# A fused two-block model kernel on one core: GpSimd's conv taps in halves, and a planner of orders with added latency and a noisy replay

## The chip, the cores and the metric

The kernel runs on one core of a Trainium2 chip. The core has five engines with queues of their own that run in order: TensorE (PE, matmuls and transposes), VectorE (DVE), ScalarE (ACT), GpSimd (POOL) and SyncE (SP, which issues DMAs; GpSimd issues some too). The metric is the device time of one execution in microseconds.

## The reference

The reference takes 512 tokens of width 1024 in float32 through two models, one behind the other. The first is one layer: an RMS norm, a mixer (a projection, a causal convolution of 4 taps, an SSD scan in chunks of 128 for 16 heads, a pooling over windows of 2 to 16 tokens, a projection), a cross-attention over 256 memory rows, a SwiGLU of width 2816, and a final norm. The second has two layers. Layer A is the one that the change touches:

```python
def conformer_conv(u, conv_w, conv_b, g, b):
    a, gl = jnp.split(u, 2, axis=-1)
    h = a * jax.nn.sigmoid(gl)
    h = jnp.pad(h, ((0, 0), (CONV_KERNEL - 1, 0), (0, 0)))      # CONV_KERNEL = 31, width 1536
    h = depthwise_conv(h, conv_w) + conv_b
    return jax.nn.silu(layer_norm(h, g, b))
```

Its output and a cross-attention over another 256 memory rows are gated, projected by `a_w_out` and added to the input, and a layer norm follows. Layer B replaces the convolution by an attention in which each query keeps the 256 keys with the best index scores.

## The kernel before, in words

Activations lie transposed, with 128 channels on the partitions and 512 tokens along a row, so one tile is 128x512. Every dense product is made of three float32r matmuls for each 128x128 block (high times high, high times low, low times high): `mm3`, called by `dense`. Weights come in through `prep` (L490): SyncE loads a raw tile (3 buffers), ScalarE rounds it to the high half, and the low half is the difference, made on VectorE with both inputs in SBUF. For the four weights named in `ADDED` (those of layer A's input projection) ScalarE writes the negated high half instead and GpSimd issues a DMA that adds the raw weight to it in SBUF.

`conv_tile` (L1190) makes one of the 12 tiles of layer A's convolution: two dense products (gate and value), the padded product `pad` on VectorE, and 31 taps. Tap 0 is scaled on ScalarE into `cg`. Taps 1 to 10 are scaled on ScalarE into a temporary `tm` each and added to `cg` by GpSimd. Tap 11 is a matmul with a diagonal, into PSUM (`cp`). Taps 12 to 30 are multiply-adds on VectorE with one input in SBUF and one in PSUM. Then `cg` and `cp` are added on VectorE, and the layer norm's running sums go to GpSimd. Beside these 12 tiles run `side` steps: the query and gate projections, the cross-attention, and a part of the output projection.

The body doesn't issue instructions. `Program.rec` (L138) records each as an `Op` with its engine, its tiles, its dependences by whole tile and an estimated duration in ns. `emit` (L402) then makes an order. `order` (L236) is a list scheduler: it walks through time, starts on each engine the ready op of least priority value, and counts the free buffers of each tag; an op is ready at its last producer's end plus `latency` (the table `LATENCY` at L53, by pair of engines). The first order takes its priorities from the program's sequence. Then `latest` (L199) walks an order backwards and gives each op a due time, the priorities become the mean of due times and old start times, and `order` runs again, 12 times (`FBI`). `replay` (L366) walks a finished sequence op by op and estimates its length; the shortest of the 13 is issued. Nothing of this runs on the chip: the chip sees only the sequence of each engine's queue, with the semaphores that the dependences need. An op flagged `port` (GpSimd's, and VectorE's where both inputs are in SBUF or the copy is a fast one) waits in the plan until the flagged op that runs on the other of the two engines has ended.

All recorded instructions are issued at L423, so the profile names them by tile and shape.

Of the kernel before, what the change touches and what calls it, by code (L numbers as in the profile page):

```python
# [26 lines left out]
SLOPES = [2.0 ** (-(i + 1)) for i in range(8)] + [2.0 ** (-0.5 * (2 * i + 1)) for i in range(4)]  # L27
BIG = 1e30
WAHEAD = 400
ADDED = ("a_gl", "a_a", "a_qm", "a_gate")  # L30
WINDOW = 1500
SSD = 600
# [10 lines left out]
for _k, _w in _VEC:  # L43
# [5 lines left out]


ENGINES = ("PE", "ACT", "DVE", "POOL", "SP")
SWITCH, FBI, LATE, REUSE, MIX = 40000, 12, 1500, 160, 0.5
LATENCY = {("PE", "PE"): 0.0, ("ACT", "ACT"): 0.0, ("DVE", "DVE"): 130.0, ("POOL", "POOL"): 102.0,  # L53
           ("PE", "ACT"): 200.0, ("PE", "DVE"): 196.0, ("ACT", "PE"): 260.0, ("DVE", "PE"): 300.0, ("POOL", "PE"): 200.0,
           ("ACT", "DVE"): 142.0, ("DVE", "ACT"): 130.0, ("ACT", "POOL"): 175.0, ("DVE", "POOL"): 190.0,
           ("POOL", "ACT"): 75.0, ("POOL", "DVE"): 60.0}
# [66 lines left out]
class Program:  # L123
# [14 lines left out]
    def rec(s, eng, fn, m, args, kw):  # L138
        o = Op()
        o.m = m  # L140
        o.eng, o.fn, o.args, o.kw, o.idx = eng, fn, args, kw, len(s.ops)
        o.prio = o.idx - s.shift
        o.outs = [args[0]] + ([kw["accum_out"]] if kw.get("accum_out") is not None else [])
        o.outs = [x.base for x in o.outs if isinstance(x, View)]
        ins = [x for x in list(args[1:]) + [v for k, v in kw.items() if k != "accum_out"] if isinstance(x, View)]
        o.ins = [x.base for x in ins]
        o.tiles = set(o.outs + o.ins)
        deps = set()
        for x in o.ins:
            if x.writer is not None:  # L150
                deps.add(x.writer)
            x.readers.append(o.idx)
        for x in o.outs:
            if x.writer is not None:
                deps.add(x.writer)
            deps.update(x.readers)
            x.writer, x.readers = o.idx, []
        deps.discard(o.idx)
        o.deps, o.succ = deps, []
        o.new = [x for x in dict.fromkeys(o.outs) if x.alloc is not None and x.left == 0]  # L160
        for x in o.tiles:
            x.left += 1
        o.port, o.table = False, None
        out = args[0]
        n = int(np.prod(out.shape[1:]))
        if eng == "PE":
            one = m == "transpose" or args[1].base.dt == F32R
            o.table = n > 8
            o.dur = 109.0 if m == "transpose" else max(112.0, n / 2.4 + 16) if one else 2 * max(111.0, n / 1.2 + 2)
        elif eng == "ACT":  # L170
            ptr = sum(isinstance(kw.get(k), View) for k in ("scale", "bias", "accum_out"))
            o.dur = n * 0.833 + 93 + 93 * ptr - 40 * (isinstance(args[1], View) and args[1].base.psum)
            o.table = _TABLE.get(args[2])
        elif eng == "DVE":
            two = m in ("tensor_tensor", "scalar_tensor_tensor")
            psum = any(x.psum for x in o.tiles)
            wide = [x for x in ins if int(np.prod(x.shape[1:])) > 1]
            ptr = len(ins) - len(wide)
            if m == "reciprocal":
                o.dur = n * 8.3 + 60  # L180
            elif m in ("tensor_reduce", "max", "match_replace"):
                o.dur = int(np.prod(wide[-1].shape[1:])) * 1.042 + 68
            elif not two and not psum:
                o.dur, o.port = n * 0.521 + 68 + 61 * ptr, n > 8
            else:
                o.dur = n * 1.042 + 68 + 61 * min(ptr, 1)
                o.port = two and sum(not x.base.psum for x in wide) == 2 and n > 8
        elif m == "dma_start" and eng == "POOL":
            o.dur, o.bytes = 1100.0, n * int(out.shape[0]) * 8 / 360.0
        elif eng == "POOL":  # L190
            o.dur, o.port = (1000 if kw.get("op") == ALU.pow else n * (2.35 if len(ins) > 1 else 1.0) + 99), n > 8
        else:
            o.dur = n * int(out.shape[0]) * 4 / 360.0
        s.ops.append(o)

    def latency(s, a, b):
        return LATENCY.get((a.eng, b.eng), 120.0)

    def latest(s, prio):  # L199

        ops = s.ops
        need = [len(o.succ) for o in ops]
        when = [0.0] * len(ops)
        ready = {e: [] for e in ENGINES}
        wait = [(0.0, -prio[o.idx], o.idx) for o in ops if not o.succ]
        heapq.heapify(wait)
        busy = dict.fromkeys(ENGINES, 0.0)
        events, port = [0.0], 0.0
        while events:
            now = heapq.heappop(events)  # L210
            while wait and wait[0][0] <= now:
                _, p, k = heapq.heappop(wait)
                heapq.heappush(ready[ops[k].eng], (p, k))
            for e, q in ready.items():
                if busy[e] > now or not q:
                    continue
                o = ops[q[0][1]]
                if o.port and port > now:
                    heapq.heappush(events, port)
                    continue  # L220
                heapq.heappop(q)
                end = now + (o.dur + 2150 if e == "SP" else o.dur + o.bytes + 2150 if o.m == "dma_start" else o.dur)
                busy[e] = now + o.dur
                if o.port:
                    port = end
                heapq.heappush(events, busy[e])
                when[o.idx] = -end
                for d in o.deps:
                    when[d] = max(when[d], end + s.latency(ops[d], o))
                    need[d] -= 1  # L230
                    if need[d] == 0:
                        heapq.heappush(wait, (when[d], -prio[d], d))
                        heapq.heappush(events, when[d])
        return when

    def order(s, prio, window):  # L236
# [28 lines left out]
        while len(seq) < len(ops):  # L265
# [5 lines left out]
            while fin and fin[0][0] <= now:  # L271
                o = ops[heapq.heappop(fin)[1]]
                for x in o.tiles:
                    left[x] -= 1
                    if left[x] == 0 and x.alloc is not None:
                        back.append((now + REUSE, x))
                        heapq.heappush(events, now + REUSE)
                for k in o.succ:
                    need[k] -= 1
                    rdy[k] = max(rdy[k], o.end + s.latency(o, ops[k]))  # L280
                    if need[k] == 0:
                        heapq.heappush(early, k)
            while back and back[0][0] <= now:
# [79 lines left out]
                    low += 1  # L363
        return seq, max(o.end for o in ops), [o.start for o in ops]

    def replay(s, seq):  # L366

        free, end, left = dict.fromkeys(ENGINES, 0.0), {}, {}
        back, taken, last = {g: [] for g in s.bufs}, dict.fromkeys(s.bufs, 0), {}
        port, hw, dma = {"POOL": 0.0, "DVE": 0.0}, 0.0, 0.0  # L370
        for o in seq:
            for x in o.tiles:
                left[x] = left.get(x, 0) + 1
        for o in seq:
            now = free[o.eng]
            for d in o.deps:
                now = max(now, end[d] + s.latency(s.ops[d], o))
            for x in o.new:
                taken[x.tag] += 1
                if taken[x.tag] > s.bufs[x.tag]:  # L380
                    now = max(now, heapq.heappop(back[x.tag]) + REUSE)
            if o.port:
                now = max(now, port["DVE" if o.eng == "POOL" else "POOL"])
            free[o.eng] = fin = now + o.dur
            if o.eng == "SP":
                hw = max(now, hw) + 470
                dma = max(hw + 650, dma) + o.dur
                fin, free["SP"] = dma + LATE, now + 470
            elif o.m == "dma_start":
                dma = max(fin + 650, dma) + o.bytes  # L390
                fin = dma + LATE
            if o.port:
                port[o.eng] = fin
            end[o.idx] = fin
            for x in o.tiles:
                left[x] -= 1
                last[x] = max(last.get(x, 0.0), fin)
                if left[x] == 0 and x.alloc is not None:
                    heapq.heappush(back[x.tag], last[x])
        return max(end.values())  # L400

    def emit(s, window):  # L402
        def real(a):
# [4 lines left out]
                s.ops[d].succ.append(o.idx)  # L408
        prio = [o.prio * 200.0 for o in s.ops]
        r = s.order(prio, window)  # L410
        best, least = r, s.replay(r[0])
        for it in range(FBI):
            w = s.latest(r[2])
            m = min(w)
            w = [MIX * (t - m) + (1 - MIX) * p for t, p in zip(w, r[2])]
            r = s.order(w, window)
            t = s.replay(r[0])
            if t < least:
                best, least = r, t
        for o in best[0]:  # L420
# [5 lines left out]
def body(ctx, tc, t, out):  # L426
# [763 lines left out]
    def conv_tile(j):  # L1190
# [14 lines left out]
        for k in range(1, NOFF):  # L1205
            tm = act(tag="tm")
            S.activation(tm, tap(k)[0], AF.Copy, scale=tap(k)[1])
            G.tensor_tensor(cg, cg, tm, op=ALU.add)
        cp = bank("B")
        if NPE:  # L1210
            for k in range(NPE):
# [378 lines left out]
```

## Time and profile before

| | us |
|---|---|
| median of 3 runs | 1716.03 |
| lowest and highest of them | 1715.26, 1717.04 |
| the profiled execution | 1714.29 |
| its span, first to last instruction | 1712.5 |
| TensorE busy in it | 1653.5 |
| VectorE busy | 1102.8 |
| ScalarE busy | 811.5 |
| GpSimd busy | 422.6 |

The profile gives the busy time of each engine, for the whole span or for stretches of it, the granted TensorE clock (1.00 is 2.4 GHz, 0.50 is 1.2 GHz), groups of instructions by form (shape) with their mean duration, and a timeline in which instructions of one form that follow each other stand in one row with their count. A bracket behind a row is the time for which the engine had nothing to do before it, and the engine and tile that ended this. A matmul's recorded duration is longer than its share of a full pipeline, so a busy TensorE isn't always one at its peak.

### The profile page before, as it was taken

How to read it: one execution, taken by the hardware profiler on the slowest of the kernel's cores; microseconds unless marked ns; L12 is line 12 of the kernel's file. 1: busy time of each engine (PE TensorE's matmuls, PEld its weight loads, DVE VectorE, ACT ScalarE, POOL GpSimd, SP SyncE). 2: the span in 40 equal slices, each digit the busy share in tenths (PEclk: the TensorE clock that was granted, in tenths of full speed). 3: DMA queues.
4: the chain of work that ended last, by engine and by line, in shares of the span. 5: the costliest groups of instructions: out<-in, count | busy, mean ns of one | idle time of the engine just before them, and what ended most of it. 6: DMA issues, size and time to landing. Idle time of an engine off the chain costs nothing. (4 is left out here: it accounts for less than half of the span.)

```text
span 1712.5 us, 21259 instructions
## 1 busy us (share of the span) xinstructions
PE 1653.5 (97%) x7950; PEld 1353.6 (79%) x7950; DVE 1102.8 (64%) x1761; ACT 811.5 (47%) x1394; POOL 422.6 (25%) x369
## 2 busy tenths in 40 slices
PE   9999998999999999999999987899799999999998
PEld 7888688888888888888888765678687788788886
DVE  7846968554664445644465996886647895467754
ACT  6623544335543222422476894674435425545541
POOL 1003532110221001101345896686230000000000
PEclk9999999999999999999999998999999999999999
DMA  7321224321333332222498625575233123111121
GB/s 235 122 86 56 93 74 125 128 92 38 111 111 99 99 98 91 95 99 78 138 219 175 142 44 132 148 166 139 97 116 114 62 87 123 61 64 50 50 86 50
DMA packets 56055, 179.39 MB, mean 105 GB/s; under 512 B 6352, under 2 KB 8272, under 8 KB 55952
## 3 DMA queue, kind: packets, MB, share of 16 engines
q1 hardware_dynamic: 49616, 154.96, 28.1%
q0 software_dynamic: 6336, 23.07, 7.6%
q8 instruction: 63, 1.03, 0.2%
q14 instruction: 40, 0.33, 0.1%
HBM read 175.78 MB, written 2.10 MB: 104 GB/s over the span
## 5 line engine op out<-in xcount | busy, mean ns | idle before, releaser
L423 PE MATMUL mm<-act,whi 128*128 128x512 f32 (+1 forms) x3888 | 1194.1, 388 | 23.8 <-DVE act L423 12.5
L423 PEld LDWEIGHTS mm<-act,whi 128*128 128x128 f32 x3888 | 720.8, 189 | 177.5 <-DVE act L423 17.3
L423 PE MATMUL mm<-act,wlo 128*128 128x512 f32 (+1 forms) x1944 | 747.5, 387 | 10.1 <-DVE wlo L423 9.9
L423 ACT ACTIVATE whi<-raw 128x1024 fp32r<-128x1024 f32 (+3 forms) x293 | 289.5, 990 | 550.4 <-PE mm L423 365.5
L423 POOL TENSOR_TENSOR act<-act,act 128x512 f32<-128x512 f32 (+1 forms) x252 | 349.9, 1437 | 625.5 <-DVE act L423 329.0
L423 PEld LDWEIGHTS mm<-act,wlo 128*128 128x128 f32 x1944 | 367.8, 189 | 84.9 <-DVE wlo L423 12.4
L423 DVE TENSOR_TENSOR wlo<-raw,whi 128x1024 fp32r<-128x1024 f32 (+3 forms) x249 | 321.8, 1294 | 121.6 <-ACT whi L423 116.7
L423 DVE TENSOR_TENSOR act<-mm,act 128x512 f32<-128x512 f32 (+3 forms) x173 | 114.6, 663 | 240.2 <-PE mm L423 234.2
L423 ACT ACTIVATE act<-act 128x512 fp32r<-128x512 f32 (+3 forms) x222 | 134.2, 617 | 130.7 <-DVE act L423 93.8
L423 DVE SCALAR_TENSOR_TENSOR B<-pad,vec,B 128x512 f32<-128x512 f32 x228 | 168.6, 753 | 11.3 <-PE B L423 6.2
L423 DVE TENSOR_TENSOR act<-act,act 128x512 f32<-128x512 f32 (+3 forms) x203 | 144.9, 742 | 32.3 <-ACT act L423 29.0
L423 POOL TENSOR_TENSOR fr<-fv,mhalf 128x1 f32<-128x1 f32 x4 | 2.2, 546 | 412.2 <-DVE fv L423 412.2
L423 PE MATMUL A<-act,act 128*128 128x256 f32 (+6 forms) x488 | 99.3, 345 | 0.6 <-ACT act L423 0.4
L423 ACT ACTIVATE act<-pad,vec 128x512 f32<-128x512 f32 x144 | 97.3, 737 | 3.0 <-DVE pad L423 2.9
L423 PEld LDWEIGHTS A<-act,act 128*128 128x128 f32 (+1 forms) x488 | 72.3, 190 | 19.7 <-issue 6.1
L423 PE MATMUL mm<-whi,act 128*128 128x512 f32 x264 | 84.3, 393 | 0.0
L423 ACT ACTIVATE act<-C 128x128 f32<-128x128 f32 (+4 forms) x164 | 52.0, 362 | 54.1 <-PE C L423 52.6
L423 PE MATMUL B<-act,act 128*128 128x128 f32 (+1 forms) x492 | 60.1, 290 | 5.4 <-DVE act L423 5.2
L423 PEld LDWEIGHTS B<-act,act 128*128 128x128 f32 (+1 forms) x492 | 50.8, 170 | 14.3 <-DVE act L423 6.3
L423 PE MATMUL C<-ident,act 128*128 128x128 f32 (+1 forms) x288 | 50.0, 279 | 9.1 <-ACT act L423 8.5
L423 PEld LDWEIGHTS mm<-whi,act 128*128 128x128 f32 x264 | 49.4, 188 | 9.6
L423 ACT ACTIVATE act<-act,vec 128x512 fp32r<-128x512 f32 (+3 forms) x68 | 46.4, 700 | 22.3 <-DVE act L423 20.8
(137 smaller groups left out, 1046.6 us busy)
## 6 DMA issues: line engine op xcount, KB each, us to landing
raw<-in_w_g_dram SPq DMA_DIRECT2D x22, 512.0 KB, 3.3
raw<-in_w_u_dram SPq DMA_DIRECT2D x22, 512.0 KB, 3.3
raw<-in_w_om_dram SPq DMA_DIRECT2D x16, 512.0 KB, 4.5
raw<-in_w_d_dram SPq DMA_DIRECT2D x16, 512.0 KB, 3.5
raw<-in_a_gate_dram SPq DMA_DIRECT2D x16, 512.0 KB, 5.5
wlo<-in_a_gate_dram POOLq DMA_DIRECT2D x16, 512.0 KB, 7.8
raw<-in_b_gate_dram SPq DMA_DIRECT2D x16, 512.0 KB, 3.3
raw<-in_b_wo_dram SPq DMA_DIRECT2D x16, 512.0 KB, 3.3
```

What stands on the lines that cost most here:

```text
L423: r = o.fn(*[real(a) for a in o.args], **{k: real(v) for k, v in o.kw.items()})
```

## The change

Three things are changed.

In `conv_tile` each of GpSimd's adds of a tap, 128x512, becomes two adds of 128x256, of the left and the right half of the columns.

The planner's numbers are changed: GpSimd's add of n columns costs 2.3 n + 80 ns (2.35 n + 99 before), a dependent GpSimd instruction has no added latency (102 ns before), the issue of an adding DMA costs 900 ns (1100 before), and its transfer 9.2 / 360 ns a 128-partition element (8 / 360 before). A load is taken to land after 1300 ns instead of 1500. There are 14 rounds instead of 12.

The planner itself is changed in two ways. `order` and `latest` use `planned`, which is the latency plus 300 ns (`SLACK`) where the two ops are on different engines. And `replay` now keeps a queue for each engine and always starts the queue head that can start first, with buffers waited for by the tiles that held them (`slots`), and with each duration but TensorE's multiplied by 1 plus 3% of the absolute value of a normal draw; `emit` judges an order by the sum over three such draws.

```diff
-SWITCH, FBI, LATE, REUSE, MIX = 40000, 12, 1500, 160, 0.5
+SWITCH, FBI, LATE, REUSE, MIX = 40000, 14, 1300, 160, 0.5
+NOISE = 3
+SLACK = 300.0
-LATENCY = {..., ("POOL", "POOL"): 102.0,
+LATENCY = {..., ("POOL", "POOL"): 0.0,
...
         elif m == "dma_start" and eng == "POOL":
-            o.dur, o.bytes = 1100.0, n * int(out.shape[0]) * 8 / 360.0
+            o.dur, o.bytes = 900.0, n * int(out.shape[0]) * 9.2 / 360.0
         elif eng == "POOL":
-            o.dur, o.port = (1000 if kw.get("op") == ALU.pow else n * (2.35 if len(ins) > 1 else 1.0) + 99), n > 8
+            o.dur, o.port = (1000 if kw.get("op") == ALU.pow else n * (2.3 if len(ins) > 1 else 1.0) + 80), n > 8
...
+    def planned(s, a, b):
+        return s.latency(a, b) + (SLACK if a.eng != b.eng else 0.0)
...
-                    when[d] = max(when[d], end + s.latency(ops[d], o))
+                    when[d] = max(when[d], end + s.planned(ops[d], o))
...
-                    rdy[k] = max(rdy[k], o.end + s.latency(o, ops[k]))
+                    rdy[k] = max(rdy[k], o.end + s.planned(o, ops[k]))
...
+    def replay(s, seq, wait, noise):
...
+            for e in live:
+                o = todo[e][0]
+                if e not in head:
+                    if any(end[d] is None for d in o.deps) or any(end[d] is None for d in wait.get(o.idx, ())):
+                        continue
+                    t = [end[d] + s.latency(ops[d], o) for d in o.deps] + [end[d] + REUSE for d in wait.get(o.idx, ())]
+                    head[e] = max(t, default=0.0)
+                t = max(head[e], free[e])
+                if o.port:
+                    t = max(t, port["DVE" if e == "POOL" else "POOL"])
+                if best is None or t < best[0]:
+                    best = (t, e)
+            now, e = best
...
+            free[e] = fin = now + o.dur * (1.0 if e == "PE" else noise[o.idx])
...
-        best, least = r, s.replay(r[0])
+        rng = np.random.default_rng(0)
+        noise = 1.0 + 0.03 * np.abs(rng.standard_normal((NOISE, len(s.ops))))
+        def judge(seq):
+            wait = s.slots(seq)
+            return sum(s.replay(seq, wait, x) for x in noise)
+        best, least = r, judge(r[0])
...
         for k in range(1, NOFF):
             tm = act(tag="tm")
             S.activation(tm, tap(k)[0], AF.Copy, scale=tap(k)[1])
-            G.tensor_tensor(cg, cg, tm, op=ALU.add)
+            for o in (0, T // 2):
+                G.tensor_tensor(cg[:, o:o + T // 2], cg[:, o:o + T // 2], tm[:, o:o + T // 2], op=ALU.add)
```

## Rows read from the trace of the kernel before

**Rows 1.** The page's head and its busy times, share of span, and counts.

```profile
span 1712.5 us, 21259 instructions
PE 1653.5 (97%) x7950; PEld 1353.6 (79%) x7950; DVE 1102.8 (64%) x1761; ACT 811.5 (47%) x1394; POOL 422.6 (25%) x369
```

**Rows 2.** Table by stage: stretch, length, busy us by engine, granted clock, DMA.

```profile
213.00:300.00 87.00, 81.86 (x571) 71.23 (x570) 68.53 (x103) 39.92 (x61) 22.05 (x17) 0.98 0.33 102
300.00:941.00 641.00, 640.17 (x2955) 531.81 (x2954) 335.04 (x419) 267.08 (x413) 118.47 (x100) 1.00 0.38 111
941.00:1037.00 96.00, 82.21 (x355) 61.26 (x354) 93.25 (x146) 82.61 (x176) 84.99 (x74) 0.96 0.39 84
1037.00:1113.00 76.00, 63.53 (x246) 48.95 (x247) 55.10 (x61) 42.96 (x60) 51.64 (x44) 0.89 0.64 157
...
1199.00:1242.00 43.00, 34.30 (x173) 28.60 (x172) 28.83 (x35) 18.98 (x32) 8.77 (x6) 0.92 0.28 97
1242.00:1307.00 65.00, 62.49 (x287) 50.78 (x285) 38.21 (x51) 28.40 (x38) 16.82 (x11) 1.00 0.33 108
1307.00:1696.00 389.00, 388.81 (x1986) 320.80 (x1986) 261.60 (x615) 174.96 (x387) 1.10 (x2) 1.00 0.22 74
1696.00:1712.50 16.50, 8.02 (x36) 6.31 (x34) 8.13 (x18) 3.04 (x8) 1.08 (x2) 0.89 0.17 65
```

**Rows 3.** The same table for the five stretches at the lower clock, with their sum.

```profile
272.00:275.40 3.40, 3.40 (x28) 3.07 (x23) 3.37 (x6) 1.36 (x4) 1.66 (x1) 0.51 0.02 5
...
1074.10:1080.90 6.80, 3.20 (x8) 2.53 (x9) 6.48 (x5) 0.00 (x0) 2.99 (x3) 0.50 0.10 39
1207.30:1214.00 6.70, 3.96 (x17) 3.70 (x17) 4.46 (x4) 6.70 (x13) 2.58 (x2) 0.50 0.04 14
sum 33.80, PE 22.04 PEld 16.97 DVE 31.07 ACT 14.00 POOL 18.06; mean PE 4.41 PEld 3.39 DVE 6.21 ACT 2.80 POOL 3.61
```

**Rows 4.** Timeline of TensorE: its three longest waits (start, us, what, idle before).

```profile
1038.94 1.65 PE L423 MATMUL mm<-act,whi 128*128 128x512 f32 x3 [6.56 <-DVE act L423]
...
1077.70 0.80 PE L423 MATMUL mm<-act,wlo 128*128 128x512 f32 x1 [8.21 <-DVE wlo L423]
...
1210.04 0.80 PE L423 MATMUL mm<-act,whi 128*128 128x256 f32 x2 [5.34 <-ACT act L423]
```

**Rows 5.** Timeline around the second of them, GpSimd and VectorE.

```profile
1067.29 1.19 POOL L423 DMA_DIRECT2D wlo<-in_a_a_dram  x1
...
1067.90 9.19 POOL L423 TENSOR_TENSOR act<-act,act 128x512 f32<-128x512 f32 x7
...
1068.36 9.29 DVE L423 TENSOR_TENSOR wlo<-raw,whi 128x512 fp32r<-128x512 f32 x1
```

**Rows 6.** Table by stage for most of the conv tiles.

```profile
940.00:1180.00 240.00, 212.26 (x904) 164.24 (x903) 192.48 (x269) 168.49 (x294) 191.06 (x164) 0.95 0.60 137
```

**Rows 7.** Groups by form, VectorE, same stretch: busy, mean ns, idle before.

```profile
L423 DVE TENSOR_TENSOR wlo<-raw,whi 128x512 fp32r<-128x512 f32 x8 | 16.3, 2062 | 0.0
L423 DVE TENSOR_TENSOR act<-act,act 128x512 fp32r<-128x512 f32 x8 | 8.1, 1056 | 0.0
...
L423 DVE TENSOR_TENSOR act<-act,act 128x512 f32<-128x512 f32 x5 | 3.3, 689 | 6.1 <-ACT act L423 3.9 <-POOL act L423 2.2
```

**Rows 8.** Timeline of GpSimd: two runs of adds.

```profile
998.51 8.16 POOL L423 TENSOR_TENSOR act<-act,act 128x512 f32<-128x512 f32 x6
...
1018.98 11.09 POOL L423 TENSOR_TENSOR act<-act,act 128x512 f32<-128x512 f32 x9 [0.84 <-ACT act L423]
```

**Rows 9.** Groups by form, GpSimd, 940 to 1180 us.

```profile
L423 POOL DMA_DIRECT2D wlo<-in_a_gl_dram x8 | 7.0, 878 | 4.6 <-ACT wlo L423 4.6
...
L423 POOL MEMSET pad<- 128x30 f32 x6 | 0.7, 124 | 6.5 <-DVE B L423 6.5
```

**Rows 10.** Timeline of GpSimd: a copy and an add into one tile.

```profile
138.27 0.19 POOL L423 COPY act<-act 128x1 f32<-128x1 f32 x1 [4.71 <-DVE act L423]
138.41 1.04 POOL L423 TENSOR_TENSOR act<-act 128x511 f32<-128x511 f32 x1
```

More of the change, by code (lines that the diff above doesn't have):

```diff
@@ L51 @@
 ENGINES = ("PE", "ACT", "DVE", "POOL", "SP")
-SWITCH, FBI, LATE, REUSE, MIX = 40000, 12, 1500, 160, 0.5
-LATENCY = {("PE", "PE"): 0.0, ("ACT", "ACT"): 0.0, ("DVE", "DVE"): 130.0, ("POOL", "POOL"): 102.0,
+SWITCH, FBI, LATE, REUSE, MIX = 40000, 14, 1300, 160, 0.5
+LATENCY = {("PE", "PE"): 0.0, ("ACT", "ACT"): 0.0, ("DVE", "DVE"): 130.0, ("POOL", "POOL"): 0.0,
            ("PE", "ACT"): 200.0, ("PE", "DVE"): 196.0, ("ACT", "PE"): 260.0, ("DVE", "PE"): 300.0, ("POOL", "PE"): 200.0,
@@ L364, in order, with slots @@
         return seq, max(o.end for o in ops), [o.start for o in ops]
[L366 to L370, printed above, removed]
+    def slots(s, seq):
+        left, users, wait = {}, {}, {}
+        back, taken = {g: deque() for g in s.bufs}, dict.fromkeys(s.bufs, 0)
         for o in seq:
@@ L374, in replay @@
         for o in seq:
-            now = free[o.eng]
-            for d in o.deps:
-                now = max(now, end[d] + s.latency(s.ops[d], o))
             for x in o.new:
@@ L380, in replay @@
                 if taken[x.tag] > s.bufs[x.tag]:
[L381 to L385, printed above, removed]
+                    wait.setdefault(o.idx, []).extend(users[back[x.tag].popleft()])
+            for x in o.tiles:
+                users.setdefault(x, []).append(o.idx)
+                left[x] -= 1
+                if left[x] == 0 and x.alloc is not None:
+                    back[x.tag].append(x)
+        return wait
+    def replay(s, seq, wait, noise):
+        ops, end, head = s.ops, [None] * len(s.ops), {}
+        todo = {e: deque(o for o in seq if o.eng == e) for e in ENGINES}
+        free, port, hw, dma = dict.fromkeys(ENGINES, 0.0), {"POOL": 0.0, "DVE": 0.0}, 0.0, 0.0
+        live = [e for e in ENGINES if todo[e]]
+        while live:
+            best = None
+            for e in live:
[11 more added lines that the diff above has]
+            now, e = best
+            del head[e]
+            o = todo[e].popleft()
+            if not todo[e]:
+                live.remove(e)
+            free[e] = fin = now + o.dur * (1.0 if e == "PE" else noise[o.idx])
+            if e == "SP":
                 hw = max(now, hw) + 470
                 dma = max(hw + 650, dma) + o.dur
-                fin, free["SP"] = dma + LATE, now + 470
+                fin, free[e] = dma + LATE, now + 470
             elif o.m == "dma_start":
@@ L392, in replay @@
             if o.port:
-                port[o.eng] = fin
+                port[e] = fin
             end[o.idx] = fin
[L395 to L400, printed above, removed]
+        return max(end)
     def emit(s, window):
@@ L416, in emit @@
             r = s.order(w, window)
-            t = s.replay(r[0])
+            t = judge(r[0])
             if t < least:
```

## The prediction, made before the change was run

> **What bounds the kernel now.** I read the page's busy times first. TensorE holds 1653.5 us of a span of 1712.5 [rows 1], so the most that any order of the same work can give is what TensorE loses: 59.0 us without an instruction, and what it loses at the lower clock. The reader is to see next, in the table by stage, that this loss is not spread out. From 300 to 941 us TensorE is idle for 0.8 us and from 1307 to 1696 for 0.2 [rows 2]: there every order is as good as another. The idle time lies at 213 to 300 (87.00 − 81.86 = 5.1 us, the SSD heads), at 941 to 1037 (13.8) and 1037 to 1113 (12.5), which are the first two thirds of the twelve conv tiles, at 1199 to 1242 (8.7, the layer norm after them), at 1242 to 1307 (2.5) and at the very end (8.5, the closing chain and the output) [rows 2].
>
> Third, the clock. Five stretches inside the kernel run at a granted clock of 0.50, so at 1.2 GHz and not 2.4; each begins during or behind an idle or thinly filled stretch of TensorE. Together they last 33.8 us and TensorE is busy in 22.0 of them; at full clock the same work would take half, so they cost 11.0 us [rows 3].
>
> Fourth, what ended the waits. The three longest are 6.56 us for an activation's low half from VectorE, 8.21 us for a weight's low half from VectorE, and 5.34 us for an evacuation on ScalarE [rows 4]. All three are in-order queues: the producer stood behind other work. The second is of a kind of its own. A VectorE subtraction of 128x512 with both inputs in SBUF took 9.29 us, from 1068.36 on, while GpSimd ran seven adds back to back from 1067.90 to 1077.09 [rows 5]. Its kind takes 0.69 us (the last group there) when nothing is in its way [rows 7]. VectorE got in between none of the seven adds.
>
> No engine is full over the whole conv stage: of 240 us, TensorE holds 212, VectorE 192, GpSimd 191, ScalarE 168 [rows 6]. VectorE alone is full in its first part (93.3 of 96.0 us, 941 to 1037) [rows 2]. So the stage is bound by the order in which four loaded in-order queues hand work to each other, and the order is what the change makes anew.
>
> **The change, part by part.**
>
> (1) *Taps in halves.* Ten adds on each of 12 tiles, 120 adds of 128x512, become 240 of 128x256. No row shows a half. A run of six adds takes 8.16 us, 1.36 each, and a run of nine 11.09, 1.23 each [rows 8]; I read the first as one tile's chain, where an add waits for the one before it, and the second as two chains mixed. An instruction with next to nothing to do, the memset of 30 columns, takes 0.124 us [rows 9]. A half is then between 1.23 / 2 = 0.615 (no fixed part) and (1.23 − 0.124) / 2 + 0.124 = 0.677 us, and two halves 1.23 to 1.35. Against a waiting add that is −0.13 to −0.01, against a mixed one 0 to +0.12: over 120 taps −16 to +14 us of GpSimd. I take 0, since runs of both kinds occur. The cover is GpSimd's idle time, 240.0 − 191.1 = 48.9 us of the stage [rows 6]; only with that gone would these microseconds reach TensorE through the sums.
>
> (2) *Who waits for the halves.* The two halves of one tap touch different columns, so they need not wait for each other, and the first half of the next tap finds its input finished one instruction ago. That GpSimd starts on another slice of a tile without waiting is in the trace: the add of 511 columns begins 0.14 us after a copy of 0.19 us into the same tile began [rows 10]. So a chain that stopped between adds (1.36) would run without a stop, as mixed ones do (1.23). That is good for GpSimd and bad for a VectorE instruction with two SBUF inputs, if rows 5 are the pattern. The stage has 8 + 8 + 5 = 21 such instructions, 27.7 us in all, where 21 × 0.69 would be 14.5 [rows 7]: 13.2 us of waiting, 8.6 of it in the one. The other twenty waited 0.2 us on average, many of them with no add in their way. One locked-out instruction costs TensorE 8.2 us of idle time [rows 4] and half of the 3.2 us that it was busy at the lower clock behind it (1.6) [rows 3], 9.8 us together. What the halves make of their number I bound by none left (−9.8) and four more (+39). I take half a one more, +5: the runs become tighter, but the planner moves the 21 instructions at the same time.
>
> [...]
>
> (3) *The planner.* The numbers in its tables cost nothing on the chip. Three kinds of edit decide the order. Each hop between engines counts 300 ns more, so a consumer is planned later behind its producer and other ready work goes in between. The replay that picks among the orders (now 15 instead of 13) starts each engine's queue head in order of time and sums three runs with durations up to some per cent longer, so an order that only just fits loses. And the costs on GpSimd's queue come nearer to the rows: a DMA's issue 0.9 instead of 1.1 us, measured 0.878 [rows 9]; an add of 512 columns 1.26 instead of 1.30 plus 0.10 for a dependent one, measured 1.23 and 1.36 [rows 8]. "Longer adding DMAs" is such a cost too; no transfer changes.
>
> What that can win: the idle time of the five stretches named above is 5.1 + 13.8 + 12.5 + 8.7 + 2.5 = 42.6 us [rows 2]; without the 8.2 of the lockout, of which the planner expects one add's length at most, 34.4. The start and the end (8.5) are chains that no order shortens. Nothing in the trace shows an order with slack, so its share lies between 0 and 34.4. The nearest rows for the upper end are the calm stages, where work stands far ahead and the loss is 1.0 us in 1030 [rows 2]; for the lower end, the full VectorE of 941 to 1037, where no order makes VectorE's 93 us shorter, only moves them. I take half, −17.2. The lower clock goes with the idle time: of its 11.0 us the lockout holds 1.6; half of the other 9.4 is −4.7.
>
> What is late next: with the 300 ns more, SBUF tiles are planned to live longer, and the 73 buffers of the `act` tag may come free later; loads of weights, which go through three raw buffers, stay where their buffers come free.
>
> **Sum.** −17.2 − 4.7 + 5 + 0 = −16.9 us on the profiled execution of 1714.29: 1697.4. That execution stands 1.74 us under the median of the runs (1716.03), so the forecast is 1699 us.
>
> **The rivals.**
>
> *Lockouts take the gain and more.* Speaking for it: rows 5, and that halves remove the stops between dependent adds. Against: twenty of 21 got in. The price is 9.8 us for each further one. With the planner's −21.9 kept, it decides from the third further one on (2.2 × 9.8 = 21.9). With four: −21.9 + 39.2 = +17.3, so 1733 us.
>
> *Slack spoils the calm stages.* An order built for late hops keeps more tiles alive and lets TensorE idle where it does not now. If the 1030 us of the calm stages came to lose as much as 1242 to 1307 does (2.5 of 65.0, 3.9%) [rows 2], that is +40 less the 1.0 there now; with −16.9 elsewhere +22, so 1738 us. Against it: those stages have VectorE at 335 of 641 us and 262 of 389, far from full.
>
> *Halves let VectorE in.* If VectorE waits for one GpSimd instruction at a time, which the twenty short waits allow and rows 5 deny, a wait ends after a half, at most 0.68 us, and no lockout is left: −17.2 − 4.7 − 9.8 = −31.7, so 1684 us.
>
> *Nearly all is won.* The three long waits of rows 4 go, three quarters of 34.4 and of 9.4 are recovered and no lockout is left: −25.8 − 7.1 − 9.8 = −42.7, so 1673 us.
>
> *The change does not do what it says.* If the halves wait for one another as whole tiles do, each pays the 0.13 us between the two pitches of rows 8, 240 × 0.13 = 31 us on GpSimd instead of nothing; 48.9 us of idle time hold most of it, but half reaching TensorE (+15.6) eats the gain: about 1715 us, within 0.2%. The same time results if the new order only moves the waits about.
>
> **How the numbers follow.** A measurement of this kernel can tell about 0.2% from no change, 3.4 us, so "same" is 1712.6 to 1719.5. Chances: the forecast's case, a part of the loss recovered, 0.40, with 1686 to 1712.6 as its own range; VectorE let in by the halves 0.14; nearly all won 0.10; no change 0.10; lockouts 0.17; calm stages spoiled 0.09. Faster is 0.40 + 0.14 + 0.10 = 0.64, same 0.10, slower 0.26. The range for 8 in 10 goes from 1676, which leaves out most of the best case, to 1736, which takes in the four further lockouts and leaves out the worse of both slow cases.
>
> **What would show it.** In the profile after, GpSimd has 240 adds of 128x256; a mean pitch between 0.61 and 0.68 us confirms (1), one near 0.75 says that halves wait. The longest VectorE subtraction with two SBUF inputs tells (2): none over 2 us says that halves let VectorE in, several over 4 us are the lockout rival. TensorE's idle time between the start of the conv tiles and the end of their layer norm, some 35 us now, should fall to about 18 for (3), and the stretches at half clock from 33.8 to about 20 us. More than 3 us of idle time in the calm stages is the slack rival. The forecast is wrong if VectorE's full stretch, not the order, made the idle time: then VectorE is again full for some 90 us and TensorE's loss beside it is the same.

## The result: slower by 1.6%, and the profile after

The changed kernel takes 1742.39 us (median of 4 runs, 1740.94 to 1747.62) where the kernel before takes 1715.99; the ratio is 1.0159, with a 95% interval of 1.0137 to 1.0181. The forecast was 1699 us, with a range up to 1736. Ratios are taken over fast executions alone, medians over all; two kernels below have one slow execution each (2760.3 us in the new planner without the halves, 1859.95 in the slack alone).

The page's head and busy times of the kernel after answer [rows 1]. The matmuls are the same 7950. The span is 28.7 us longer, and TensorE's idle time grows from 59.0 to 1741.2 − 1659.7 = 81.5 us.

```profile
span 1741.2 us, 21393 instructions
PE 1659.7 (95%) x7950; PEld 1358.9 (78%) x7950; DVE 1136.3 (65%) x1761; ACT 817.8 (47%) x1398; POOL 441.4 (25%) x489
```

The table by stage of the kernel after (stretch, length, busy us of PE, PEld, DVE, ACT and POOL with counts, granted clock, DMA) answers [rows 2], and its last row, a sum over the nine stretches at the lower clock (granted 0.50 to 0.51), [rows 3].

```profile
300.00:860.00 560.00, 560.00 (x2610) 468.51 (x2610) 284.29 (x351) 211.39 (x337) 78.41 (x59) 1.00 0.31 99
...
950.00:1045.00 95.00, 73.29 (x299) 57.32 (x299) 84.38 (x102) 65.26 (x121) 66.42 (x95) 0.87 0.51 114
1045.00:1150.00 105.00, 85.52 (x323) 63.63 (x322) 90.77 (x90) 51.84 (x95) 75.07 (x92) 0.89 0.41 99
1150.00:1250.00 100.00, 88.62 (x411) 71.78 (x410) 75.31 (x92) 62.26 (x89) 70.06 (x70) 0.98 0.54 132
...
1340.00:1724.00 384.00, 383.96 (x1972) 317.10 (x1971) 257.88 (x610) 174.66 (x384) 1.11 (x2) 1.00 0.22 74
...
sum 54.40, PE 39.55 PEld 30.17 DVE 44.98 ACT 24.64 POOL 21.96; mean PE 4.39 PEld 3.35 DVE 5.00 ACT 2.74 POOL 2.44
```

The calm stages are as calm as before. Most of the added loss is in the conv tiles and the layer norm after them: 21.7, 19.5 and 11.4 us of TensorE's idle time in three stretches of some 100 us, 52.6 together, where the stage from 941 to 1242 us lost 36.4 before (13.79 + 12.47 + 8.70 by [rows 2], and 1.48 in the stretch left out there). If half the clock means half the pace, an estimate from the granted 0.50, the lower clock costs half of the 39.6 us that TensorE was busy in it, 19.8, where it cost 11.0. In the traces of both kernels matmuls of 512 columns mostly start 0.427 us apart in these stretches (1.2 columns a ns; the views give the clock as a share only) and 0.227 us apart at 1.00, so by the matmuls it is 47% rather than half.

The timeline of VectorE in the kernel after (start, us, what, idle before), its longest instructions, answers the third row of [rows 5]:

```profile
959.03 3.53 DVE L457 TENSOR_SCALAR xm<-xm 128x2 f32<-128x2 f32 x1
...
987.09 6.90 DVE L457 TENSOR_SCALAR xm<-xm 128x2 f32<-128x2 f32 x1
...
1017.42 9.85 DVE L457 TENSOR_SCALAR xm<-xm 128x2 f32<-128x2 f32 x1
...
1067.81 8.66 DVE L457 TENSOR_TENSOR act<-act,act 128x512 fp32r<-128x512 f32 x2
...
1100.02 5.05 DVE L457 TENSOR_TENSOR wlo<-raw,whi 128x512 fp32r<-128x512 f32 x1 [3.34 <-PE mm L457]
...
1126.16 15.94 DVE L457 TENSOR_TENSOR wlo<-raw,whi 128x512 fp32r<-128x512 f32 x1
```

The first three scale two columns of maxima, an instruction whose quickest copy takes 0.16 us. The fourth row holds two instructions; the long one is the second, 7.79 us. Together the six rows take 49.9 us; undisturbed they would take about 3 (four subtractions at 0.69, three scalings at 0.16). GpSimd's timeline beside them, kernel after:

```profile
958.67 0.80 POOL L457 DMA_DIRECT2D wlo<-in_a_a_dram  x1
959.29 2.96 POOL L457 TENSOR_TENSOR act<-act,act 128x256 f32<-128x256 f32 x4
...
986.21 0.81 POOL L457 DMA_DIRECT2D wlo<-in_a_gl_dram  x1
986.82 7.14 POOL L457 TENSOR_TENSOR act<-act,act 128x256 f32<-128x256 f32 x10
...
1016.20 1.00 POOL L457 DMA_DIRECT2D wlo<-in_a_gl_dram  x1
1016.82 9.43 POOL L457 TENSOR_TENSOR act<-act,act 128x256 f32<-128x256 f32 x13
...
1068.08 0.97 POOL L457 DMA_DIRECT2D wlo<-in_a_gate_dram  x1
1068.69 7.22 POOL L457 TENSOR_TENSOR act<-act,act 128x256 f32<-128x256 f32 x10
...
1125.66 0.87 POOL L457 DMA_DIRECT2D wlo<-in_a_a_dram  x1
1126.28 9.23 POOL L457 TENSOR_TENSOR act<-act,act 128x256 f32<-128x256 f32 x13
1135.27 1.08 POOL L457 DMA_DIRECT2D wlo<-in_a_gl_dram  x1
1135.88 5.67 POOL L457 TENSOR_TENSOR act<-act,act 128x512 f32<-128x512 f32 x6
```

Each long VectorE instruction begins at most 2.1 us away from such a run's start and ends at most 1.1 us behind its end: 987.09 + 6.90 = 993.99 beside 986.82 + 7.14 = 993.96. Five of the runs begin with halves; the one beside 1100.02 is five adds of 512 columns, up to a gap at 1104.51. (A row carries the shape of its first instruction: the last one above is two adds of 512 columns and four of 256.) All six begin right behind a DMA that GpSimd issues, the one beside 1100.02 behind a DMA at 1097.35; so did the run of [rows 5]. And TensorE waits for each, by its timeline in the kernel after:

```profile
963.74 1.65 PE L457 MATMUL A<-act,act 128*128 128x256 f32 x6 [4.17 <-ACT act L457]
...
999.35 0.77 PE L457 MATMUL mm<-act,whi 128*128 128x512 f32 x1 [5.86 <-DVE pad L457]
...
1039.01 2.05 PE L457 MATMUL B<-pad,act 128*128 128x512 f32 x2 [8.75 <-DVE pad L457]
...
1076.53 0.79 PE L457 MATMUL mm<-act,whi 128*128 128x512 f32 x1 [5.07 <-DVE act L457]
...
1105.81 0.47 PE L457 MATMUL mm<-act,whi 128*128 128x512 f32 x1 [2.71 <-DVE act L457]
...
1142.16 0.80 PE L457 MATMUL mm<-act,wlo 128*128 128x512 f32 x1 [8.74 <-DVE wlo L457]
```

That is 35.3 us in six waits. Four of them name another engine or tile than the long instruction: at 963.74 ScalarE's exponentials had waited for the scaling, at 999.35 and 1039.01 `pad`, and at 1105.81 an activation's low half, stood in VectorE's queue behind it. The kernel before has one such wait [rows 4].

### The profile page after: what moved, and what is told of

The parts are those of the page before. It is cut to its first block, busy times and chain, and to the rows that moved or that the text cites. A ratio compares the mean times of both kernels' runs of the same rounds, so it can differ in the third digit from the quotient of the medians.

```text
span 1741.2 us, 21393 instructions
## 1 busy us (share of the span) xinstructions
PE 1659.7 (95%) x7950; PEld 1358.9 (78%) x7950; DVE 1136.3 (65%) x1761; ACT 817.8 (47%) x1398; POOL 441.4 (25%) x489
## 5 line engine op out<-in xcount | busy, mean ns | idle before, releaser
L457 POOL TENSOR_TENSOR act<-act,act 128x256 f32<-128x256 f32 (+2 forms) x372 | 367.1, 1133 | 624.1 <-DVE act L457 331.2
L457 PEld LDWEIGHTS mm<-act,wlo 128*128 128x128 f32 x1944 | 368.7, 190 | 91.0 <-DVE wlo L457 12.4
L457 DVE TENSOR_TENSOR wlo<-raw,whi 128x1024 fp32r<-128x1024 f32 (+3 forms) x249 | 334.4, 1343 | 140.1 <-ACT whi L457 120.8
L457 ACT ACTIVATE act<-act 128x512 fp32r<-128x512 f32 (+2 forms) x222 | 133.5, 616 | 108.1 <-DVE act L457 72.3
L457 DVE TENSOR_TENSOR act<-act,act 128x512 fp32r<-128x512 f32 (+3 forms) x203 | 148.5, 763 | 22.0 <-ACT act L457 19.0
L457 PE MATMUL B<-act,act 128*128 128x128 f32 (+2 forms) x492 | 61.0, 294 | 0.5 <-DVE act L457 0.5
L457 ACT ACTIVATE act<-mm 128x512 f32<-128x512 f32 (+3 forms) x92 | 51.6, 563 | 1.1 <-PE mm L457 1.0
```

Source lines behind the costliest of these rows:

```text
L457: r = o.fn(*[real(a) for a in o.args], **{k: real(v) for k, v in o.kw.items()})
```

## The experiments

The theory after this reading: the halves, by leaving no stop between adds, lock VectorE out, and this costs more than the new order wins. The rival: the new order is bad by itself, and the long instructions are only where its trouble shows. The first four kernels part the order from the halves. Two keep an order and exchange the halves; the other queues keep their order, instruction by instruction. Times are medians; ratios are to the kernel before, run beside them on the same chip (1714.9 to 1715.6 us). The edits are shown shortened.

**The changed order with whole adds.** The two halves of a tap are issued as one add, in the place of the second.

```diff
-G.tensor_tensor(cg[:, o:o + T // 2], cg[:, o:o + T // 2], tm[:, o:o + T // 2], op=ALU.add)   # for both halves
+G.tensor_tensor(cg, cg, tm, op=ALU.add)        # when issued; planned as two halves
```

> The order of the changed kernel on all queues, with each pair of half adds issued as one add of 128x512 in the place of the second half. Lockout theory (halves let GpSimd run without a stop and keep VectorE off the shared inputs): the six VectorE instructions that took 3.5 to 15.9 us are gone, at most two over 3 us are left, TensorE loses the 35 us of waiting behind them and some 8 us at the lower clock, so 1697 to 1710 us. Order theory (the new order is bad by itself, halves are harmless): 1737 to 1747 us, with the same waits of TensorE.

Measured: 1709.4 us, ratio 0.9959 (0.9945 to 0.9973). Not one queue's order was touched, and 33 us are gone. The order theory falls. Two VectorE instructions of 2.23 and 5.36 us are left in the conv tiles.

**Halves, in alternating order.** On every second tap the right half is added first, so each tap's first add works on the half that was just written and must wait for it.

```diff
 for o in (0, T // 2):
+    e = o if k % 2 else T // 2 - o
-    G.tensor_tensor(cg[:, o:o + T // 2], ...)
+    G.tensor_tensor(cg[:, e:e + T // 2], ...)
```

> The changed kernel with one edit: on every second tap the right half is added first, so that the add behind it, which works on the same half, must wait for the one just before it. Same instructions, same sizes, same order of tiles. Lockout theory: a stop at each tap boundary lets VectorE in after two halves (about 1.4 us); no VectorE instruction over 3 us in the conv tiles, 1697 to 1715 us. If it is the number or cost of the halves, or the order, that costs the time: 1737 to 1750 us, since each stop adds 0.1 us.

Measured: 1710.39 us, ratio 0.9974 (0.9959 to 0.9988). The same number and size of instructions, in the same places, only a stop once a tap: 32 us less. It isn't the number or the cost of the halves. With the stops a run of 13 halves takes GpSimd 10.48 us where it takes 9.43 in the changed kernel, and the time doesn't show this. One VectorE instruction over 3 us is left where none was expected: a subtraction of 5.36 us, beside five adds of 512 columns that follow a DMA and aren't taps.

**The old order with halves.**

```diff
-G.tensor_tensor(cg, cg, tm, op=ALU.add)
+for c in (0, T // 2):                           # when issued; planned as one add
+    G.tensor_tensor(cg[:, c:c + T // 2], cg[:, c:c + T // 2], tm[:, c:c + T // 2], op=ALU.add)
```

> The kernel before, in its own order, with each tap's add issued as two halves. Lockout theory: VectorE instructions of over 3 us appear where the chains had stopped until now, several of them, and the time rises to 1728 to 1750 us. Order theory: 1713 to 1719 us.

Measured: 1723.68 us, ratio 1.0052 (1.0035 to 1.0069), between the ranges of the two theories. The timeline of VectorE in this kernel shows the old long subtraction and two new long instructions:

```profile
988.76 4.22 DVE L428 TENSOR_SCALAR xm<-xm 128x2 f32<-128x2 f32 x1
...
1073.15 9.70 DVE L428 TENSOR_TENSOR wlo<-raw,whi 128x512 fp32r<-128x512 f32 x1
...
1100.13 3.97 DVE L428 TENSOR_TENSOR wlo<-raw,whi 128x512 fp32r<-128x512 f32 x1
```

So the halves cost 9 us in the old order (1723.7 − 1715.0) and 33 in the new one (1742.4 − 1709.4): two more long instructions there, five here. How many VectorE instructions fall beside a long run is a matter of the order.

**The new planner without the halves,** planned and issued as whole taps.

```diff
-for o in (0, T // 2):
-    G.tensor_tensor(cg[:, o:o + T // 2], cg[:, o:o + T // 2], tm[:, o:o + T // 2], op=ALU.add)
+G.tensor_tensor(cg, cg, tm, op=ALU.add)
```

> The changed planner with whole taps, planned and issued as such: the change without the halves. Lockout theory: 1697 to 1716 us. Order theory: 1730 to 1747 us.

Measured: 1698.82 us, ratio 0.9895 (0.9877 to 0.9913). The planner's part of the change makes the kernel 16 us faster; its longest waiting scaling takes 1.9 us.

**The small scaling, one column at a time.** Three of the six are an instruction of two columns that my forecast hadn't counted.

```diff
-V.tensor_scalar(mx, mx, sc, -1.0, op0=ALU.mult, op1=ALU.mult)                                     # 128x2
+for c in (0, 1):
+    V.tensor_scalar(mx[:, c:c + 1], mx[:, c:c + 1], sc, -1.0, op0=ALU.mult, op1=ALU.mult)         # 128x1
```

> The changed kernel in its own order, with the small scaling of the attention's maxima (128x2, SBUF to SBUF, VectorE) issued as two instructions of one column each. If an even column count is what makes this form wait for GpSimd, the three of them that took 3.5, 6.9 and 9.9 us shrink to about 0.2 us, TensorE's waits of 4.2, 5.9 and 8.8 us behind them go with about 6 us at the lower clock, and the time is 1714 to 1726 us; the three long subtractions stay. If any SBUF-to-SBUF scaling waits, 1738 to 1747 us with the same long instructions.

Measured: 1726.84 us, ratio 1.0067 (1.0052 to 1.0082), 16 us less than the changed kernel and 0.8 us above the range that was expected. The two answers on tile `xm` (VectorE; minimum, median and maximum in ns), first of the changed kernel and then of this one:

```profile
L457 DVE TENSOR_SCALAR xm<-xm x6: 160/2226/9847, 951.8 to 1017.4; 128x2 f32<-128x2 f32 x6
```
```profile
L461 DVE TENSOR_SCALAR xm<-xm x12: 142/146/149, 952.3 to 1008.4; 128x1 f32<-128x1 f32 x12
```

With two columns this instruction took up to 9.85 us beside GpSimd's adds; with one, and the queues in the same order, none of its 12 copies took more than 0.149. The pairs at 959.10 and 961.38 us took 0.21 us each; in the changed kernel GpSimd's four adds run from 959.29 to 962.25. The long subtractions are still there (15.95 us the longest).

**One stop behind each of GpSimd's DMAs.** All seven locked-out instructions of the two kernels lie beside a run that a DMA begins. This kernel is the changed one with two copies of one column behind each of the 44 adding DMAs; the second reads what the first writes, so GpSimd stops once there (for 0.05 to 0.07 us between the two, from 950 to 1040 us), and the halves stay independent.

```diff
 r = o.fn(...)
+if o.eng == "POOL" and o.m == "dma_start":
+    nc.gpsimd.tensor_copy(scr1, mhalf)
+    nc.gpsimd.tensor_copy(scr2, scr1)
```

> The changed kernel in its own order, with two copies of one column put behind each of GpSimd's 44 adding DMAs, the second reading what the first wrote, so that GpSimd stops once behind each DMA; the halves stay independent of each other. All six long VectorE instructions of the changed kernel lie beside a run of adds that begins right behind such a DMA. If the run without a stop that the DMA starts is what keeps VectorE off: no VectorE instruction over 3 us, 1705 to 1720 us (the copies cost GpSimd some 20 us, off the path). If independent halves keep VectorE off by themselves: the long instructions stay, 1738 to 1752 us.

Measured: 1702.64 us, ratio 0.993 (0.9913 to 0.9946): 88 instructions more, 40 us less, and 2.4 us under the expected range. The groups by form of VectorE from 940 to 1200 us (count, busy us, mean ns, idle before), first in the changed kernel, then here, answer [rows 7]:

```profile
L457 DVE TENSOR_TENSOR wlo<-raw,whi 128x512 fp32r<-128x512 f32 x8 | 27.4, 3420 | 3.3 <-PE mm L457 3.3
L457 DVE TENSOR_SCALAR xm<-xm 128x2 f32<-128x2 f32 x6 | 22.0, 3670 | 0.0
L457 DVE TENSOR_TENSOR act<-act,act 128x512 fp32r<-128x512 f32 x8 | 13.9, 1762 | 0.0
```
```profile
L457 DVE TENSOR_TENSOR act<-act,act 128x512 fp32r<-128x512 f32 x12 | 13.1, 1121 | 0.0
L457 DVE TENSOR_TENSOR wlo<-raw,whi 128x512 fp32r<-128x512 f32 x8 | 9.4, 1170 | 2.3 <-issue 2.3
L457 DVE TENSOR_SCALAR xm<-xm 128x2 f32<-128x2 f32 x6 | 1.8, 307 | 0.0
```

A run of halves with a stop before it lets VectorE in. The timelines of GpSimd and VectorE in this kernel have runs as long as ever, and the scalings beside them are short; beside the four halves shown last, a scaling of the changed kernel took 3.53 us:

```profile
949.84 9.13 POOL L457 TENSOR_TENSOR act<-act,act 128x256 f32<-128x256 f32 x13
...
959.51 0.40 POOL L459 COPY scr<-mhalf 128x1 f32<-128x1 f32 x1
959.97 0.19 POOL L460 COPY scr<-scr 128x1 f32<-128x1 f32 x1
960.12 2.80 POOL L457 TENSOR_TENSOR act<-act,act 128x256 f32<-128x256 f32 x4
```
```profile
951.85 0.16 DVE L457 TENSOR_SCALAR xm<-xm 128x2 f32<-128x2 f32 x1
...
958.65 0.35 DVE L457 TENSOR_SCALAR xm<-xm 128x2 f32<-128x2 f32 x1
...
960.92 0.63 DVE L457 TENSOR_SCALAR xm<-xm 128x2 f32<-128x2 f32 x1
```

So it is not independence alone. In each of the seven long cases GpSimd had gone from a DMA's issue straight into adds that don't wait. The changed kernel has a case of its own that differs in this:

```profile
948.50 0.89 POOL L457 DMA_DIRECT2D wlo<-in_a_gate_dram  x1 [4.08 <-ACT wlo L457]
949.61 9.11 POOL L457 TENSOR_TENSOR act<-act,act 128x256 f32<-128x256 f32 x13 [0.21 <-ACT act L457]
```

Here GpSimd waited 0.21 us for ScalarE behind the DMA, and the scaling at 951.80 took 0.66 us.

Runs that lock VectorE out can also be told from the record of GpSimd alone, where the times of its instructions overlap. Of the 13 adds from 1016.82 on, each starts 0.39 to 0.46 us before the recorded end of the instruction ahead; in the run at 949.61 above it is 0.03. The changed kernel has 14 runs of three or more instructions that overlap by more than 0.1 us, each begun by a DMA. In the kernel with the stops, from 950 to 1040 us, no run of adds ends more than 0.07 us behind the start of what follows it. The condition isn't complete: in such runs of the changed kernel four more instructions, at 934.77, 1059.28, 1067.81 and 1197.64, all in or just before a DMA's issue, took only 0.54 to 0.95 us. And whether the stop matters, or only the 0.6 us that the copies put before the adds, was not tested.

**What in the planner wins.** Four kernels vary it, all with whole taps, and one joins the single-column scaling to the best of them.

```diff
-SLACK = 300.0
+SLACK = 0.0                                     # and 150.0, and 600.0, in kernels of their own
```

> The changed planner with whole taps and a slack of 0 instead of 300 ns. If the added latency made the gain of the planner over the kernel before (1699 against 1715 us): 1709 to 1720 us, with TensorE waiting more often and for short times. If the new replay and costs made it: 1694 to 1704 us.

> The changed planner with whole taps and half the slack, 150 ns. If the slack itself buys time, the result lies between that with 0 (1721 us) and that with 300 (1699 us): 1704 to 1716 us. If each slack only draws another order, it can lie anywhere from 1698 to 1722 us, outside that as easily as inside.

> The changed planner with whole taps and twice the slack, 600 ns. If slack buys time up to a point, near 300: 1696 to 1710 us. If the calm stages pay for the longer lives of tiles: TensorE idles there by more than 3 us. If each slack only draws another order: anywhere from 1698 to 1722 us.

Measured: 1721.49 us with 0 (ratio 1.004, 1.0026 to 1.0054), 1702.48 with 150 (0.9931, 0.9914 to 0.9948), 1698.82 with 300 and 1715.75 with 600 (1.0004, 0.9994 to 1.0014). The first lies 1.5 us above the range expected if slack buys time, the second 1.5 us below its range, and the last only in the range of another order. With 0 no VectorE instruction is locked out for long (the longest takes 2.24 us where it should take 0.7), so its loss is one of order: TensorE's waits in that kernel (us in total, times, longest) are those that slack is meant for.

```profile
PE mm L457 <- DVE act L457: 14.6, 6, 6.7
PE mm L457 <- ACT act L457: 14.3, 9, 3.9
PE B L457 <- DVE act L457: 11.1, 4, 5.9
```

With 600 the calm stages stay calm (0.6 us idle from 320 to 850 us), so tiles held longer isn't what costs there; two subtractions of 7.5 and 3.8 us are a part of it, and the rest was not pursued.

```diff
 # kernel before: costs, replay and whole taps as they were
-when[d] = max(when[d], end + s.latency(ops[d], o))
+when[d] = max(when[d], end + s.planned(ops[d], o))
-rdy[k] = max(rdy[k], o.end + s.latency(o, ops[k]))
+rdy[k] = max(rdy[k], o.end + s.planned(o, ops[k]))
```

> The kernel before with the 300 ns added in planning alone: its costs, replay and whole taps stay. If the added latency made the gain: 1694 to 1705 us. If the replay and the costs made it: 1711 to 1720 us.

Measured: 1712.64 us, ratio 0.9988 (0.9978 to 0.9998). It looks as if slack won nothing here, but this order meets the lockout with whole taps: of VectorE's timeline in this kernel

```profile
993.45 4.28 DVE L428 TENSOR_SCALAR xm<-xm 128x2 f32<-128x2 f32 x1
...
1067.88 11.44 DVE L428 TENSOR_TENSOR wlo<-raw,whi 128x512 fp32r<-128x512 f32 x1
...
1101.20 5.00 DVE L428 TENSOR_TENSOR wlo<-raw,whi 128x512 fp32r<-128x512 f32 x1
```

and TensorE waits 22.2 us for low halves of weights, against 9.9 in the kernel before. The expectation's two answers were too simple: what an order wins and what it loses to lockouts add up in one time.

```diff
-("POOL", "POOL"): 0.0
+("POOL", "POOL"): 102.0
```

> The changed planner with whole taps and the 102 ns between dependent GpSimd adds put back, which the zero of the changed table leaves out for whole taps. If the planner's gain is more than the luck of one order, another order under nearly the same numbers is again faster than the kernel before: 1692 to 1706 us. If it was luck: 1710 to 1725 us.

Measured: 1710.6 us, ratio 0.9975 (0.9966 to 0.9984). It is faster than before by 4 us, but this lies in the range expected if the gain of the planner was the luck of one order: 12 us lie between two orders whose planning differs by 102 ns in one entry. One run of the planner is one draw.

**The best.** The order of the planner with whole taps, and the scaling by single columns.

```diff
 # the new planner without the halves, and:
-V.tensor_scalar(mx, mx, sc, -1.0, op0=ALU.mult, op1=ALU.mult)
+for c in (0, 1):
+    V.tensor_scalar(mx[:, c:c + 1], mx[:, c:c + 1], sc, -1.0, op0=ALU.mult, op1=ALU.mult)
```

> The changed planner with whole taps, in the order of that kernel, with the scaling of the attention's maxima as two single-column instructions. Its two-column form took 1.9 us at the longest there, so little is to be won: 1693 to 1700 us if even short waits of these reach TensorE, 1697 to 1701 us if they are covered.

Measured: 1693.86 us, ratio 0.9885 (0.987 to 0.99). It beats both kernels; against the same order with two columns (0.9877 to 0.9913) the intervals overlap, so the scaling's share isn't shown.

## Why the prediction was wrong

**What bounds the kernel** held. The calm stages stayed calm, most of the loss stayed in the conv tiles and their norm, and the lower clock went with the waits (33.8 us at 0.50 before, 54.4 after).

**Step (1), the halves' cost, was a little too low and did no harm.** Runs of halves take 7.14 / 10 = 0.71 us each, above the 0.615 to 0.677 that I gave. GpSimd's busy time rose by 441.4 − 422.6 = 18.8 us, where the bounds were −16 to +14. That its idle time covers this is shown by the kernel with a stop behind each DMA: there GpSimd is busy for 464.1 us, more still, and the time is 1702.6.

**Step (2), the lockouts, is the step that failed.** The mechanism was named, with its price and its place, as a rival with 17%; the forecast took "half a one more, +5". It measured +33 (against whole adds in the same order) to +40 (against a stop behind each DMA). What was mis-sized is the number: the kernel before has one lockout, the changed kernel six. The price was not too low. Whole adds removed five of the six and the stops all of them, so one cost 33 / 5 or 40 / 6, 6.6 us, where I had taken 9.8. Three things were wrong in the step. First, the count: I counted the 21 subtractions with two inputs in SBUF and left out the eight scalings of 128x2, which run from SBUF to SBUF as well. The kernel before already showed them waiting, at 1.67 us for the longest where 0.16 is its shortest (its line is below), and they made three of the six lockouts and 16 of the microseconds. Second, the length: I priced each at the one case seen, but the six run from 3.53 to 15.94 us, and a second DMA can carry one on. The longest spans 13 halves, a DMA and six adds behind it. Third, the reason: I argued from the twenty short waits that VectorE mostly gets in, while [rows 5] had in its first row what set the one long case apart, GpSimd's DMA right before the run. The program has 44 such DMAs, 28 of them in the stretch of [rows 6]; with whole taps they had led to one lockout, so that row spoke for more than 17% but didn't settle the number. The scalings of the kernel before, on tile `xm` (VectorE; minimum, median and maximum in ns):

```profile
L423 DVE TENSOR_SCALAR xm<-xm x8: 156/608/1672, 940.0 to 1003.2; 128x2 f32<-128x2 f32 x8
```

The rival's 39 us for four further lockouts is close to what five cost. That its 1733 us was still 9 too low lies with step (3).

In the kernel with the stops no 128x512 subtraction or add of VectorE took more than 1.80 us, which is its own 0.69 and less than one add of 512 columns (1.23): that fits a wait for one instruction at most. Behind a DMA issue without a stop it doesn't fit: one subtraction took 15.94 us beside 19 adds.

**Step (3), the planner, had about the right size in another order, and was too large in this one.** The forecast was −17.2 − 4.7 = −21.9; measured without the halves, 1698.82 − 1715.0 = −16.2. But planning with halves gave a different order. That order is worth 1709.4 − 1715.0 = −5.6 with whole adds, and 1702.64 − 1715.0 = −12.4 with the stops, which also take away the lockout that the kernel before has. So of the 43 us by which the forecast missed, 28 to 35 are step (2)'s and 10 to 16 are this step's. Half of what looked movable was a choice, and the kernels with other slacks show its spread: from −16 to +7 us. The 1721, 1702 and 1699 us at 0, 150 and 300 ns speak for slack, but 600 ns gave 1716, these are one order each, and the order with 102 ns put back differs from its neighbour by 12 us. So which share is the slack's, the replay's and the costs' stays open. It also stays open why this planner sent six instructions into runs of halves; its `port` flag lets VectorE in after each add, and doesn't know of the two-column scaling (it exempts all instructions of at most 8 columns).

**The other rivals.** The calm stages weren't spoiled, at 300 ns nor at 600. The halves don't wait for one another: in the run at 949.61 us they follow each other at 0.70 us, and each begins 0.03 us before the recorded end of the one ahead. "Halves let VectorE in" came true in one kernel, the one with a stop behind each DMA (1.80 us the longest).

## What to carry to other kernels

In this kernel a VectorE instruction was held up for a whole run of GpSimd's adds, 15.94 us at the longest, where the run followed a DMA issue and had no stop in it, and halves, which made GpSimd's stream smoother, cost the time 33 us. So when an edit smooths one engine's stream, look in the timeline for the longest copy of a form, not at its mean, and for what the other engine did just before. A stop (an instruction that waits for the one before it) behind each DMA cost GpSimd half a microsecond here ((464.1 − 441.4) / 44) and gave back 40 us. And try the parts of a bundle of edits alone: here the planner alone wins 16 us and the halves lose 33 in its order.

## What the runs showed of the hardware that was not expected

- A 128x512 instruction of VectorE with two SBUF inputs, or a scaling of 128x2, could be held back for as long as GpSimd ran adds without a stop behind a DMA issue: 6.90 us for 10 halves, 9.85 for 13, 15.94 across 13 halves, a DMA and further adds. With a stop behind each DMA none of these took more than 1.80 us. Why a DMA's issue begins such a run was not shown.
- A scaling of two columns from SBUF to SBUF waits like that (9.85 us for 256 numbers at the longest), one of a single column did not (0.142 to 0.149 us in 12 of 12, with the queues in the same order). No run here has another count, and why the two differ was not shown.
- GpSimd's adds of 256 columns follow each other at 0.70 to 0.73 us (13 in 9.11 and in 9.43), those of 512 at 1.23 to 1.36 [rows 8]; cutting an add in two costs up to about 0.2 us, an estimate (2 × 0.73 − 1.23).
